# One broadcast add on VectorE and one wide absolute value in place of 16 small activations in the delta rule's decay exponent

## The chip, the cores and the metric

The kernel runs on one core of a Trainium2 chip. The core has five engines with a queue of their own each: TensorE (PE, matrix products; its weight loads are PEld), VectorE (DVE), ScalarE (ACT), GpSimd (POOL) and SyncE (SP, which issues the DMAs here). The metric is the device time of one execution in microseconds (us), less is better.

## The reference

One layer of a diffusion backbone on 1024 latent tokens and 256 context tokens of width 1024: a norm and modulation, one wide input projection, a Fourier branch and a bidirectional gated DeltaNet branch of 8 heads, gates and an output projection, then a convolutional feed-forward part. The change lies in the DeltaNet branch. Cut to that:

```python
gc = jnp.cumsum(chunks(g), axis=-1)                       # log-decay, summed within a chunk
decay = jnp.exp(jnp.where(lower_incl, gc[..., :, None] - gc[..., None, :], -jnp.inf))
l_mat = jnp.where(lower_strict, bc[..., :, None] * kk * decay, 0.0)
sol = lax.linalg.triangular_solve(l_mat, rhs, ...)        # per chunk
qk = jnp.einsum('nbhcd,nbhsd->nbhcs', qc, kc) * decay
state, o = lax.scan(step, state, (q_head, qk, u, w, k_tail, g_last))   # chunk by chunk
```

The kernel takes chunks of 128 tokens and needs, for each chunk and each of the two directions, the 128 x 128 table exp(-|gc_i - gc_j|).

## The kernel before

**Recording and planning.** The program is written as a list of operations; line 349 (`issue`) emits every one of them, so all instructions of the profile carry that line. Before that a list scheduler (`schedule`) orders them: each operation has a cost in ns by a formula (`cost`), a rank from its longest chain of followers, and the engine that comes free first takes the ready operation of the highest rank. Each engine then runs its list strictly in that order. An operation's cost, its engine and their number thus set the order of all that is recorded around it, on every queue.

**Stages.** The DeltaNet part has ten stages, in the order c0, x0, x1, c1, x2, ... x7 (`ORDER`): c0 and c1 take four heads of the context each (4 heads x 2 chunks), x0 to x7 one head of the latent tokens each (8 chunks). So a stage always has NU = 8 blocks of 128 x 128 per direction d, in one tile of 128 x 1024. One stage is

- `decay_products`: for each direction d the chunk sums are loaded as a row, broadcast over the 128 partitions, into a tile `F` (512 KB, four buffers, two per stage); for each block u an activation takes the absolute value of the row plus a bias (`gcol`, minus the chunk sums, one number per partition and block); one activation of 1024 columns takes exp(-F). Then k k^T on TensorE, times F on VectorE (`L`), and q k^T times F;
- `invert_blocks`: 62 small VectorE operations between two round trips through DRAM (`dl` out, `bl` in; `dtt` out, `k2` in);
- `merge_blocks`: some 100 small matmuls with VectorE, ScalarE and GpSimd between them, giving the inverse `N`;
- `scan_head` or `scan_ctx`: the chain over the chunks. For a latent head it needs `qh`, the query times exp of the chunk sums (one activation of 1024 columns and one VectorE product for each direction).

`decay_products` of stage i + 1 is recorded before the scan of stage i, the inverse and the merge after it. Around them stand independent products of 512 columns (projections of k, v, q, z, the gates and f: `project_kv`, `project_kq`, `sides`), which TensorE runs while a stage's chain waits. Their results leave PSUM through ScalarE (`zh...` for z, `xsv...` for v, `qT...` for q), two banks in turn. I call the stretch between the end of one scan and the start of the next a **turn**, and name it by the stage whose F is made in it. After the ten stages come the Fourier part, the merge of the branches and the feed-forward part (from about 950 us on).

The pieces that the prediction's steps touch: lines 800 to 809 (F), 811 to 814 (k k^T, bank `pd`), 1103 to 1108 (qh), 978 to 980 (k of the context, loaded back from DRAM by `kq_ctx` after `project_kv` has stored it), 1142 to 1150 (z and the gates leave PSUM).

Of the kernel before, what the change touches and what calls it, by code (L numbers as in the profile page):

```python
# [11 lines left out]
AF = mybir.ActivationFunctionType  # L12
ALU = mybir.AluOpType
# [3 lines left out]
P = 128  # L17
# [470 lines left out]
def layer(prog, a, out):  # L488
    te, ve, se, po, sp = (prog.eng[n] for n in ("PE", "DVE", "ACT", "POOL", "SP"))
# [13 lines left out]
    def ps(tag, shape, name):  # L503
        return psum.tile(shape, F32, tag=tag, name=name, bufs=PPB if tag == "pp" else 1)
# [64 lines left out]
    def dt(tag, name, shape=(P, T), dtype=F32):  # L569
        return dp.tile(list(shape), dtype, tag=tag, name=name, bufs=bufs.get(tag, 1))  # L570
# [218 lines left out]
    NU = 8  # L789
# [6 lines left out]
    def decay_products(name, kT, co, cols, growsrc, qT=None):  # L796
        rk, b2, bk, c1 = co
        gcol = cols(ngc)
        Fs, LTs = [], []
        for d in range(2):  # L800
            F_ = dt("F", f"F_{name}{d}", (P, NU, P))
            src = growsrc(d)
            Ff = F_.rearrange("p u j -> p (u j)")
            sp.dma_start(Ff.rearrange("p (a b) -> p a b", a=src.shape[1]) if len(src.shape) == 3 else Ff, src)
            for u in range(NU):
                se.activation(F_[:, u, :], F_[:, u, :], AF.Abs, bias=gcol[:, d, u:u + 1])
            se.activation(F_, F_, AF.Exp, scale=-1.0)
            Fs.append(F_)
            LTs.append(dt("LT", f"L_{name}{d}", (P, NU, P)))
        for g in range(2):  # L810
            pt = ps("pd", [P, 4, P], f"kk_{name}{g}")
            for i in range(4):
                u = g * 4 + i
                te.matmul(pt[:, i, :], kT[:, u * P:(u + 1) * P], kT[:, u * P:(u + 1) * P], start=True, stop=True)
            for d in range(2):
                for i in range(4):
                    u = g * 4 + i
                    ve.scalar_tensor_tensor(LTs[d][:, u, :], pt[:, i, :], b2[:, d, u:u + 1], Fs[d][:, u, :],
                                            op0=ALU.mult, op1=ALU.mult)
        cl = dt("CL", f"CL_{name}", (P, 2 * NU, 32))  # L820
        for b in range(4):
            se.activation(cl[bnd[b], 0:NU, :], LTs[0][bnd[b], :, bnd[b]], AF.Copy)
            ve.transpose(cl[bnd[b], NU:2 * NU, :], LTs[1][bnd[b], :, bnd[b]])
        dl = dram.tile([2 * NU, P, 32], F32, tag="dl", name=f"dl_{name}", bufs=2)
        sp.dma_start(dl.rearrange("u p j -> p u j"), cl)
        if qT is not None:
            for g in range(2):
                pt = ps("pd", [P, 4, P], f"qkp_{name}{g}")
                for i in range(4):
                    us = slice((g * 4 + i) * P, (g * 4 + i + 1) * P)  # L830
                    te.matmul(pt[:, i, :], kT[:, us], qT[:, us], start=True, stop=True)
                for d in range(2):
                    fs = Fs[d][:, 4 * g:4 * g + 4, :]
                    ve.tensor_tensor(fs, pt, fs, op=ALU.mult)
            for d in range(2):
                po.affine_select(out=Fs[d], in_=Fs[d], pattern=[[0, NU], [1 - 2 * d, P]], compare_op=ALU.is_ge,
                                 fill=0.0, base=0, channel_multiplier=2 * d - 1)
        return Fs, LTs, dl
# [188 lines left out]
    def prepare_ctx(p, kT, rk, qT, qn):  # L1027
        made = {}

        def cols(t):  # L1030
            if id(t) not in made:
                g = const.tile([P, 2, 4, 2], F32, tag=f"g_{len(made)}", name=f"g_{len(made)}{p}", bufs=2)
                po.tensor_copy(g, t[:, :, 4 * p:4 * p + 4, 8:10])
                made[id(t)] = g.rearrange("p d h c -> p d (h c)")
            return made[id(t)]
        co = coefs(f"c{p}", rk, cols)
        src = lambda d: grd3[d * 8 + 4 * p:d * 8 + 4 * p + 4, 8:10, :].rearrange(
            "(o i) c j -> o i (c j)", o=1).broadcast_to([P, 4, TC])
        return co, cols, decay_products(f"c{p}", kT, co, cols, src)
# [54 lines left out]
    def prepare_head(h, kT, rk, qT, qn):  # L1094
        def cols(t):
            return t[:, :, h, 0:8]
        co = coefs(f"x{h}", rk, cols)
        return co, cols, decay_products(f"x{h}", kT, co, cols, grow_rows(h), qT)
# [155 lines left out]
    for g4 in range(NF):  # L1254
# [12 lines left out]
        for odd in range(2):  # L1267
            ve.tensor_tensor(quad[:, 0, odd, 0:1], ft[:, 0:1], ft[:, HALF:HALF + 1],
                             op=ALU.subtract if odd else ALU.add)
# [528 lines left out]
```

## Time and profile before

| what | value |
|---|---|
| time, median of 3 runs | 2051.59 us (2049.98 to 2053.32) |
| the profiled execution | 2047.95 us, its span 2046.2 us |
| busy PE / PEld | 1953.0 us (95%) / 1570.9 us (77%) |
| busy DVE / ACT / POOL | 1363.1 us (67%) / 858.1 us (42%) / 564.0 us (28%) |
| chain that ended last | PE 71%, DVE 14%, DMA 5%, ACT 5% |
| mean granted TensorE clock | 0.979 of full speed |

Busy time is what the profiler saw an engine work; matmuls overlap each other, so 95% does not mean that TensorE does all it could. A row of the timeline gives start and length in us, the engine, the operation, output<-input (m is a tile in SBUF, p one in PSUM, d one in DRAM), the shape, how many instructions were put together (x8), and in brackets how long the engine was idle before it and whose end released it.

### The profile page before, as it was taken

To read this page: it belongs to the slowest core of one execution; us is meant where nothing else is said; L and a number is where in the kernel's file an instruction comes from. 1 tells how busy PE (TensorE), PEld (TensorE's weight loads), DVE (VectorE), ACT (ScalarE), POOL (GpSimd) and SP (SyncE) were. 2 spreads that over 40 slices of the span, in tenths; PEclk is the share of its full clock that TensorE was granted. 3 is DMA by queue.
4 is the path that set the end of the run, shared out by engine and by line. 5 is a ranking of instruction groups with operands and counts; after the bars stand their busy time and mean duration, and the time that the engine had idled before them with its cause. 6 is when DMAs were issued, how large, how long until landed. Compare 5 with 4: busy or idle time off the path is not lost.

```text
span 2046.2 us, 31495 instructions
## 1 busy us (share of the span) xinstructions
PE 1953.0 (95%) x11470; PEld 1570.9 (77%) x11470; DVE 1363.1 (67%) x2848; ACT 858.1 (42%) x2088; POOL 564.0 (28%) x573
## 2 busy tenths in 40 slices
PE   8989999899999999999999999979999999999998
PEld 3868888787777788778776778857878888878886
DVE  5648767667677577673655485479988889882132
ACT  5575354555354453632431032454444444532121
POOL 3110121101112220210221000257878888600000
PEclk9989999899999999999999999999999999999999
DMA  7153324344451543441778562312222222453231
GB/s 298 52 187 92 105 88 132 117 145 128 113 149 52 149 150 92 118 114 51 223 234 289 181 221 102 114 52 78 95 75 80 83 83 86 167 181 100 77 126 52
DMA packets 180637, 257.52 MB, mean 126 GB/s; under 512 B 75921, under 2 KB 97522, under 8 KB 180482
## 3 DMA queue, kind: packets, MB, share of 16 engines
q1 hardware_dynamic: 180482, 255.51, 39.0%
q8 instruction: 90, 1.47, 0.3%
q14 instruction: 65, 0.53, 0.1%
HBM read 194.52 MB, written 60.94 MB: 125 GB/s over the span
## 4 chain that ended last, share of the span: by engine, by line
PE 71%; DVE 14%; DMA 5%; ACT 5%; issue 2%; POOL 1%; SPq 0%; DVEq 0%; POOLq 0%; ACTq 0%
PE p L349 71%; DVE m L349 11%; ACT m L349 4%; DMA m<-d 3%; DVE p L349 3%; DMA d<-m 2%; ACT p L349 1%; POOL m L349 1%; DMA m<-in_w_ada_dram 1%; SPq L349 0%; DMA m<-in_wu_dram 0%; ACT L349 0%; DVEq L1787 0%; POOLq L1787 0%; DVEq L349 0%
## 5 line engine op out<-in xcount | busy, mean ns | idle before, releaser
L349 PE MATMUL p<-m,m 128*128 128x512 f32 (+7 forms) x11310 | 1937.8, 338 | 75.7 <-ACT m L349 31.6
L349 PEld LDWEIGHTS p<-m,m 128*128 128x128 f32 (+4 forms) x11310 | 1551.2, 174 | 452.6 <-ACT m L349 62.4
L349 DVE TENSOR_TENSOR m<-m,m 128x512 fp32r<-128x512 f32 (+27 forms) x1096 | 557.4, 523 | 253.4 <-ACT m L349 222.8
L349 ACT ACTIVATE m<-m 128x512 fp32r<-128x512 f32 (+8 forms) x649 | 411.3, 652 | 613.5 <-DMA m<-d 161.0
L349 POOL TENSOR_TENSOR m<-m,m 128x512 fp32r<-128x512 f32 (+5 forms) x338 | 449.5, 1353 | 782.6 <-DVE m L349 625.1
L349 ACT ACTIVATE m<-p 128x512 f32<-128x512 f32 (+5 forms) x510 | 221.1, 448 | 329.3 <-PE p L349 286.0
L349 DVE SCALAR_TENSOR_TENSOR m<-p,m,m 128x128 f32<-128x128 f32 (+4 forms) x488 | 203.1, 452 | 92.3 <-ACT m L349 40.9
L349 DVE SCALAR_TENSOR_TENSOR p<-m,m,p 128x512 f32<-128x512 f32 x352 | 240.1, 749 | 2.7 <-ACT p L349 0.4
L349 ACT ACTIVATE m<-p,m 128x128 f32<-128x128 f32 (+2 forms) x240 | 115.7, 495 | 184.3 <-PE p L349 179.5
L349 POOL MEMSET m<- 128x1024 f32 (+7 forms) x79 | 35.7, 460 | 381.7 <-PE p L349 224.0
L349 POOL COPY m<-m 32x256 f32<-32x256 f32 (+2 forms) x136 | 60.3, 447 | 211.5 <-DMA m<-d 173.7
L349 DVE SCALAR_TENSOR_TENSOR m<-m,m 128x512 f32<-128x512 f32 (+5 forms) x119 | 65.7, 558 | 28.6 <-ACT m L349 16.3
L349 DVE COPY m<-p 32x256 f32<-32x256 f32 (+11 forms) x116 | 42.1, 368 | 62.5 <-PE p L349 32.8
L349 DVE TENSOR_TENSOR m<-p,m 128x512 f32<-128x512 f32 (+4 forms) x91 | 57.8, 645 | 30.5 <-PE p L349 29.1
L349 DVE SCALAR_TENSOR_TENSOR m<-m,m,m 128x1024 f32<-128x1024 f32 (+2 forms) x68 | 59.6, 878 | 26.0 <-DMA m<-in_w_ada_dram 25.6
L349 DVE TENSOR_TENSOR m<-m,p 128x128 f32<-128x128 f32 (+3 forms) x117 | 53.4, 458 | 29.6 <-PE p L349 28.8
L349 ACT ACTIVATE p<-p 128x128 f32<-128x128 f32 x208 | 55.4, 266 | 25.6 <-PE p L349 23.6
L349 DVE SCALAR_TENSOR_TENSOR m<-m,p 128x512 f32<-128x512 f32 x76 | 50.7, 682 | 13.9 <-ACT m L349 7.7
L349 DVE SCALAR_TENSOR_TENSOR m<-m,m,p 128x128 f32<-128x128 f32 x128 | 42.7, 342 | 23.5 <-PE p L349 22.8
L349 ACT ACTIVATE m<-m,m 128x128 f32<-128x128 f32 (+1 forms) x168 | 54.6, 406 | 6.3 <-DMA m<-d 3.6
L349 POOL TENSOR_SCALAR_AFFINE_SELECT m<-m 128x1024 f32<-128x1024 f32 x16 | 18.9, 1199 | 100.4 <-DVE m L349 100.4
L349 DVE SCALAR_TENSOR_TENSOR m<-m 128x1 f32<-128x1 f32 (+1 forms) x25 | 4.7, 188 | 54.3 <-ACT m L349 54.2
(20 smaller groups left out, 210.3 us busy)
## 6 DMA issues: line engine op xcount, KB each, us to landing
m<-d SPq DMA_DIRECT2D x76, 512.0 KB
d<-m SPq DMA_DIRECT2D x138, 256.0 KB
m<-d SPq DMA_DIRECT2D x114, 256.0 KB
m<-in_wi_dram SPq DMA_DIRECT2D x106, 256.0 KB
m<-in_w_ada_dram SPq DMA_DIRECT2D x48, 512.0 KB
m<-in_wu_dram SPq DMA_DIRECT2D x88, 256.0 KB
m<-in_wn_dram SPq DMA_DIRECT2D x26, 512.0 KB
m<-d SPq DMA_DIRECT2D x44, 192.0 KB
```

Source lines behind the costliest of these rows:

```text
L349: return getattr(engine.real, method)(*[real(v) for v in args], **{k_: real(v) for k_, v in kw.items()})
```

## The change

For each direction of each stage, the eight activations of 128 columns (16 per stage) go. In their place one VectorE addition of 1024 columns adds `gcol`, broadcast along the 128 columns of each block, in place on F, and one activation of 1024 columns takes the absolute value. The exponential after it stays.

```diff
-            for u in range(NU):
-                se.activation(F_[:, u, :], F_[:, u, :], AF.Abs, bias=gcol[:, d, u:u + 1])
+            ve.tensor_tensor(F_, F_, gcol[:, d, :].rearrange("p (u o) -> p u o", o=1).broadcast_to([P, NU, P]), op=ALU.add)
+            se.activation(F_, F_, AF.Abs)
             se.activation(F_, F_, AF.Exp, scale=-1.0)
```

Over ten stages ScalarE has 140 instructions less and VectorE 20 more; no DMA and no matmul is added or taken away. The planner gets other costs, and so the order changes on every engine from shortly before the first stage to the end of the last one; from the middle of the products with w_dn (`mf`, line 1402) on it is the same again.

ScalarE's queue at turn x4. The 128x128 rows of x8 are the absolute values of the two F tiles (m_191, m_197), m_241 and m_267 are the two `qh` of stage x3, p_126 is the bank from which a z product leaves. Before:

```order
 L349 ACTIVATE p_173,m_1115<-p_173 128x128
 L349 ACTIVATE m_191<-m_191,m_1051 128x128 x8
 L349 ACTIVATE m_197<-m_197,m_1051 128x128 x8
 L349 ACTIVATE m_191<-m_191 128x1024
 L349 ACTIVATE m_197<-m_197 128x1024
 L349 ACTIVATE m_354<-p_173 8x128
 L349 ACTIVATE m_241<-m_241 128x1024
 L349 ACTIVATE m_267<-m_267 128x1024
 L349 ACTIVATE m_3823<-m_3884 128x512
 L349 ACTIVATE m_4380<-p_126 128x512
```

And now, on the same engine at the same turn:

```order
 L349 ACTIVATE m_241<-m_241 128x1024
 L349 ACTIVATE m_354<-p_173 8x128
 L349 ACTIVATE m_4300<-p_126 128x512
 L349 ACTIVATE m_191<-m_191 128x1024
 L349 ACTIVATE m_267<-m_267 128x1024
 L349 ACTIVATE m_197<-m_197 128x1024
 L349 ACTIVATE m_191<-m_191 128x1024
 L349 ACTIVATE m_197<-m_197 128x1024
 L349 ACTIVATE m_518<-p_124,m_328 128x512
 L349 ACTIVATE m_4300<-p_126 128x512
```

One `qh` exponential and one z product's way out of PSUM now stand ahead of all work on F, the second `qh` between the two absolute values.

VectorE's queue at the same turn, with the change. m_744 is the block inverse of stage x3, whose last step is the 128x16 row; m_241 and m_267 are the `qh` products; m_191 and m_197 are the new additions; the SCALAR_TENSOR_TENSOR on m_354 is a first step of the scan of x3, the transpose the first step of its merge:

```order
 L349 TENSOR_TENSOR m_744<-m_744,m_737 128x16
 L349 TENSOR_TENSOR m_241<-m_518,m_241 128x1024
 L349 TENSOR_TENSOR m_191<-m_191,m_1032 128x1024
 L349 TENSOR_TENSOR m_197<-m_197,m_1032 128x1024
 L349 SCALAR_TENSOR_TENSOR m_354<-p_169,m_1042,m_207 128x128
 L349 TENSOR_TENSOR m_267<-m_518,m_267 128x1024
...
 L349 STREAM_TRANSPOSE m_773<-m_423 128x512
```

Without the two additions the queue before had the same rows in the same order: the additions stand behind the finished inverse and ahead of the first scan step and the merge.

TensorE's queue at the first stage. p_97<-m_284 is k k^T of c0, which reads the loaded k; p_124 and p_126 are the two halves of the first v product. Before:

```order
 L349 MATMUL p_124<-m_115,m_479 128x512
 L349 MATMUL p_124<-m_200,m_479 128x512
 L349 MATMUL p_124<-m_115,m_507 128x512
 L349 MATMUL p_97<-m_284 128x128 x4
 L349 MATMUL p_126<-m_401,m_497 128x512
 L349 MATMUL p_126<-m_120,m_497 128x512
```

Now:

```order
 L349 MATMUL p_126<-m_91,m_507 128x512
 L349 MATMUL p_126<-m_115,m_479 128x512
 L349 MATMUL p_97<-m_284 128x128 x4
 L349 MATMUL p_126<-m_200,m_479 128x512
 L349 MATMUL p_126<-m_115,m_507 128x512
```

The k k^T products moved behind 22 of the 24 products of the second half (p_126), which they stood ahead of.

## Rows read from the trace of the kernel before

**Rows 1.** The page: busy time, and the clock in 40 slices (tenths).

```profile
PE 1953.0 (95%) x11470; PEld 1570.9 (77%) x11470; DVE 1363.1 (67%) x2848; ACT 858.1 (42%) x2088; POOL 564.0 (28%) x573
PEclk9989999899999999999999999999999999999999
```

**Rows 2.** Who waited for whom, 100 to 1100 us: total us, times, longest.

```profile
PE p L349 <- ACT m L349: 16.9, 13, 4.2
PE p L349 <- DMA m<-d: 14.3, 7, 8.7
```

**Rows 3.** Groups by shape: count | busy us, mean ns | idle before.

```profile
L349 ACT ACTIVATE m<-m,m 128x128 f32<-128x128 f32 x160 | 50.5, 397 | 3.6 <-DMA m<-d 3.6
L349 ACT ACTIVATE m<-m 128x1024 f32<-128x1024 f32 x46 | 47.1, 1056 | 10.2 <-DMA m<-d 5.0 <-DMA m<-in_x_dram 3.2 <-DMA m<-in_ctx_dram 1.8
L349 DVE TENSOR_TENSOR m<-m,m 128x1024 f32<-128x1024 f32 x36 | 44.5, 1248 | 13.0 <-ACT m L349 12.6
```

**Rows 4.** Timeline of ACT, turn x2, in order of time.

```profile
470.54 4.50 ACT L349 ACTIVATE m<-m,m 128x128 f32<-128x128 f32 x15
474.94 2.00 ACT L349 ACTIVATE m<-m 128x1024 f32<-128x1024 f32 x2
...
477.11 0.68 ACT L349 ACTIVATE m<-p,m 128x512 f32<-128x512 f32 x1
477.68 0.59 ACT L349 ACTIVATE m<-p 128x512 f32<-128x512 f32 x1
```

**Rows 5.** Timeline of PE, the same turn.

```profile
472.62 2.24 PE L349 MATMUL p<-m,m 128*128 128x512 f32 x9
478.33 2.29 PE L349 MATMUL p<-m,m 128*128 128x512 f32 x5 [3.47 <-ACT m L349]
```

**Rows 6.** Timeline of ACT, turn x4.

```profile
602.18 2.46 ACT L349 ACTIVATE m<-m,m 128x128 f32<-128x128 f32 x8 [2.69 <-DMA m<-d]
604.94 2.46 ACT L349 ACTIVATE m<-m,m 128x128 f32<-128x128 f32 x8 [0.30 <-DMA m<-d]
607.29 2.00 ACT L349 ACTIVATE m<-m 128x1024 f32<-128x1024 f32 x2
609.18 0.25 ACT L349 ACTIVATE m<-p 8x128 f32<-8x128 f32 x1
609.34 2.50 ACT L349 ACTIVATE m<-m 128x1024 f32<-128x1024 f32 x3
611.75 0.57 ACT L349 ACTIVATE m<-p 128x512 f32<-128x512 f32 x1
```

**Rows 7.** Timelines of PE and DVE, the same turn.

```profile
612.38 1.22 PE L349 MATMUL p<-m,m 128*128 128x512 f32 x2 [4.18 <-ACT m L349]
610.41 1.23 DVE L349 TENSOR_TENSOR m<-m,m 128x1024 f32<-128x1024 f32 x1 [8.90 <-ACT m L349]
```

**Rows 8.** Timelines of ACT and PE, turn x5.

```profile
674.24 4.79 ACT L349 ACTIVATE m<-m,m 128x128 f32<-128x128 f32 x16
678.92 2.01 ACT L349 ACTIVATE m<-m 128x1024 f32<-128x1024 f32 x2
681.74 2.71 PE L349 MATMUL p<-m,m 128*128 128x512 f32 x6 [2.47 <-ACT m L349]
```

**Rows 9.** The first stage: PE's timeline, then two pieces of the chain (start, us).

```profile
147.25 1.01 PE L349 MATMUL p<-m 128*128 128x128 f32 x3 [8.74 <-DMA m<-d]
132.48 8.47 DMA d<-m
141.01 5.50 DMA m<-d
```

**Rows 10.** Windows: length, PE, PEld, DVE, ACT, POOL busy (x), clock, DMA share, GB/s.

```profile
142.70:156.40 13.70, 8.63 (x27) 7.07 (x28) 6.78 (x24) 13.69 (x39) 2.45 (x3) 0.50 0.47 154
477.20:484.00 6.80, 5.67 (x14) 4.31 (x15) 4.04 (x7) 3.24 (x6) 1.64 (x1) 0.50 0.62 116
610.30:624.00 13.70, 7.93 (x139) 5.45 (x140) 6.88 (x11) 4.37 (x9) 6.46 (x12) 0.50 0.29 75
682.00:685.40 3.40, 3.40 (x9) 2.68 (x9) 1.75 (x3) 2.15 (x4) 1.90 (x2) 0.50 0.72 154
```

**Rows 11.** Timeline of DVE: two wide products one behind the other.

```profile
398.35 2.36 DVE L349 TENSOR_TENSOR m<-m,m 128x1024 f32<-128x1024 f32 x2
```

## Prediction

> **What bounds the kernel now.** The page comes first: TensorE is busy for 95% of the span, VectorE for 67%, ScalarE for 42% [rows 1]. So an edit on ScalarE and VectorE moves the end only where TensorE waits for them, and the whole prize lies in TensorE's idle time and in the stretches in which its clock is down. The view of waits for 100 to 1100 us, where the ten stages run, says how much that is: TensorE waited 16.9 us for ScalarE's tiles and 14.3 us for loads from DRAM [rows 2]. Next, the timelines at the longest of these waits. Three of the ScalarE waits, 3.47, 4.18 and 2.47 us, together 10.1 us, fall in the turns x2, x4 and x5 [rows 5, 7, 8], and in each ScalarE is in the middle of the very activations that the change takes out: 15 or 16 absolute values in a row of 4.5 to 4.9 us, and two exponentials of 2.0 us behind them [rows 4, 6, 8]. TensorE waits there for nothing in F; it waits for a PSUM bank, and the activation that empties it (477.11 and 477.68, 611.75) is queued behind F [rows 4, 6]. The longest load wait, 8.74 us, is k k^T of the first stage: the store of k took 8.47 us, and loading it back 5.50 [rows 9]. Last the windows: after four of these waits the granted clock reads 0.50, the lower of the two levels, for 13.7, 6.8, 13.7 and 3.4 us, with TensorE busy for 8.63, 5.67, 7.93 and 3.40 us of them [rows 10]; half of such busy time is lost.
>
> **What each edit costs.** Durations first. Fifteen absolute values end to end take 4.50 us, one alone 0.397, so one takes (4.50 - 0.40) / 14 = 0.293 us of ScalarE's time [rows 3, 4] and eight take 2.34. A wide one without bias takes 2.00 - 1.06 = 0.94 us when another follows [rows 3, 4]. ScalarE so saves 2.34 - 0.94 = 1.40 us per direction, 20 x 1.40 = 28 us in all. No row shows a VectorE addition with this broadcast; the nearest are its products of 1024 columns, 1.25 us in the mean and 2.36 - 1.23 = 1.13 end to end [rows 3, 7, 11]. I take 1.25: VectorE gains 20 x 1.25 = 25 us. Latency on one tile hardly moves: 2.34 + 0.94 before, 1.25 + 0.94 + 0.94 and a hand-over now. So F isn't ready sooner; what changes is how long ScalarE is shut for others.
>
> One rule of the Trainium skill speaks against the edit. The rows price a biased absolute value of 128 columns at 0.293 us of queue time [rows 3, 4]. In "ScalarE: Activation LUTs", section "What ACT_TABLE_LOAD costs", a bias read per partition adds about 93 ns to an activation: an estimate by that page makes the bias itself worth 160 x 0.093 = 15 us of ScalarE in all. By that sum alone the change would buy an addition of 15 us on one engine with 25 us on another. The rows include what that sum leaves out, that seven of eight fixed costs go too, and no run here has shown the bias apart.
>
> *The three turns.* At x2 and x5, 16 absolute values and two exponentials shut ScalarE for 6.3 to 6.7 us [rows 4, 8]. By the order, three wide activations (2.8 us) now stand ahead of the first bank's exit at x2, and at x4 and x5 one z exit stands ahead of all of F. x2: 6.3 - 2.8 = 3.5 us earlier, of a wait of 3.47; I take -3.0. x4: the exit at 611.75 waited for the landing of F (2.69 and 0.30 us), for F and for two `qh` [rows 6]; one exit is now free of that, the second isn't, and the first `qh` product, for which VectorE sat 8.90 us [rows 7], can run before F lands. I take -3.5 of 4.18. x5: -2.0 of 2.47. Together -8.5; bounds 0 (the banks fill again at once, the second exit waits as before) and -10.1.
>
> *The clock behind them.* TensorE was busy 5.67 + 7.93 + 3.40 = 17.0 us at the lower level [rows 10]; if none of it came back, 8.5 us would be won. I take half, -4; bounds 0 and -8.5.
>
> *The opening.* k k^T moves behind 22 products of 512 columns. Nine take 2.24 us, the last alone some 0.4, so one takes 0.23 [rows 5] and 22 take 5.1. Against that, one addition now stands on VectorE between the second and third pieces of the key that must be stored: +1.25, if its row has landed by then. Net -3.9, I take -4. Bounds: 0 (the store and the load land as much later) and, with the clock after it, -8.7 - 8.63 / 2 = -13.0 [rows 9, 10].
>
> *The additions' place.* At x4, x5 and x6 they stand behind the finished inverse, where VectorE before sat idle 8.90 us [rows 7]; that wait is their cover, and there I cost them at nothing. At c1, x2 and x3 they stand amid a merge, an inverse and a scan: two additions each delay such a chain by 2 x 1.13 = 2.3 us [rows 11]. I charge two of the three, +4.5. Bounds 0 and, all 20 uncovered, +25. Where a row lands late (2.69 + 0.30 us at x4 [rows 6]) VectorE is now held as well, and ScalarE behind it; as the rest of the order is also new, I charge one such landing, +3, bounds 0 and +9 for three. SyncE issues the same transfers; nothing there is dearer.
>
> **Sum.** -8.5 - 4 - 4 + 4.5 + 3 = -9.0 us. The profiled execution took 2047.95 us, 1.75 more than its span, and would take 2039.0; it lies 3.6 us under the median of 2051.59. From the median the forecast is **2042.6 us**. The bounds added up would be -31.6 and +34; they don't all meet.
>
> **The rivals.** *No change: loads set the turns.* At x4 F landed at 602.18 and 604.94 [rows 6], later than ScalarE wanted it. If the landings and not ScalarE's queue decide, the waits stay, first on VectorE and then on ScalarE; then only x2 is won (-3.0), the +3 takes it back, and the opening stays as it is: 0, or about 2051.6. For it: 14.3 us of waits for loads [rows 2]. Against: at x2 and x5 the absolute values ran without a wait for a load [rows 4, 8].
>
> *Slower: VectorE's queue is the one that is late.* VectorE runs in order; an addition that waits for its row holds the scan's first step and the merge's transpose behind it, and the merge ends the stage. Price: 2.3 us for a stage, and 3.0 for a late landing. It decides from where VectorE's idle time in a turn is under 2.3 us. If five of the ten stages lose their 2.3, two of them wait for a landing too, half of the three turns' gain and the opening's stay and the clock gives nothing back: 11.5 + 6.0 - 4.25 - 4 = +9.25, or 2060.8. For it: VectorE was busy 67% [rows 1], ScalarE only 42. Against: the 8.90 us of VectorE idle at the turn [rows 7]. What this rests on is also stated by the Trainium skill, "Perfetto Trace Analysis", section "Per-engine timelines": the queues of ScalarE, VectorE and GpSimd are strictly first in, first out. The trace agrees: at 602.18 ScalarE had sat 2.69 us before one load, and nothing behind it ran [rows 6].
>
> *Faster still: the opening closes.* If the first load lands before TensorE reaches k k^T, its 8.74 us and the low clock go with it: -13.0 in place of -4, 2033.6.
>
> That the change doesn't do what it says is out: the order shows the wide operations in place of the small ones.
>
> **How the numbers follow.** Forecast (2036 to 2047.4) 0.45, opening closed (2028 to 2036) 0.15, loads set the turns (2047.5 to 2055.7) 0.20, VectorE late (2055.7 to 2070) 0.20. 0.2% is 4.1 us, about what a measurement of this kernel can tell from no change: faster by more 0.60, within 0.20, slower 0.20. The range of 8 in 10 leaves out the lower part of the opening's case (0.06) and the upper part of the slow one (0.13): 2031 to 2059.
>
> **What the profile after would show.** Right: ScalarE about 28 us less busy and VectorE 25 us more; 20 additions of 1.1 to 1.4 us; no ScalarE wait of TensorE over 2.5 us at x2, x4 and x5, the `qh` product of x3 before F's addition; less time at the lower clock between 477 and 685 us; the first long wait under 6 us. Wrong: TensorE's waits for VectorE's tiles grow by as much as those for ScalarE's shrink, or additions with several us of idle ahead of them for a load while a transpose or scan step stands behind; or new waits for loads at places where before had none, since the whole list was planned anew. The last would make the prediction wrong without touching its reasons, and is the reason why the range is wide.

## The result, and the profile after

The changed kernel takes **2031.31 us** (median of 4 runs, 2029.80 to 2035.48) against 2052.45 for the kernel before beside it: a ratio of **0.9896, 95% interval 0.9878 to 0.9915**, some 21 us less. The forecast was 2042.6, with a range of 2031 to 2059. The direction was right, the gain was more than twice the 9.0 us forecast, and the time lies at the very edge of the range. The profiled execution took 2029.80 us, span 2028.1.

The page of the kernel after: busy time and the clock in 40 slices. It answers to [rows 1].

```profile
PE 1947.3 (96%) x11470; PEld 1566.6 (77%) x11470; DVE 1383.4 (68%) x2868; ACT 829.1 (41%) x1948; POOL 560.0 (28%) x573
PEclk9999999899999999999999999999999999999999
```

ScalarE is 29.0 us less busy (forecast 28), VectorE 20.3 us more (25). TensorE's waits from 100 to 1100 us, after, answer to [rows 2]:

```profile
PE p L349 <- ACT m L349: 15.0, 18, 2.4
PE p L349 <- DVE m L349: 10.6, 16, 2.3
PE p L349 <- ACT p L349: 8.2, 5, 4.1
PE p L349 <- DMA m<-d: 2.0, 3, 1.1
```

No wait for ScalarE's tiles in SBUF (the m) is over 2.4 us, yet their total fell only from 16.9 to 15.0 us: the three turns fell by 4.3 us (10.1 to 5.8), and waits at other places grew. The waits for loads fell from 14.3 to 2.0 us, and 4.1 us of that came back at the opening as a wait for ScalarE (ACT p). The turns, after; first x2, ACT and then PE, for [rows 4, 5]:

```profile
471.08 3.10 ACT L349 ACTIVATE m<-m 128x1024 f32<-128x1024 f32 x3 [0.45 <-DVE m L349]
474.08 0.67 ACT L349 ACTIVATE m<-p,m 128x512 f32<-128x512 f32 x1
474.65 1.04 ACT L349 ACTIVATE m<-m 128x1024 f32<-128x1024 f32 x1
475.60 0.58 ACT L349 ACTIVATE m<-p 128x512 f32<-128x512 f32 x1
476.23 6.12 PE L349 MATMUL p<-m,m 128*128 128x512 f32 x19 [2.31 <-ACT m L349]
```

Three wide activations stand ahead of the first bank's way out of PSUM (its exit, for short), as the prediction read from the order, and a fourth between it and the second exit (475.60), with whose end the wait ends. TensorE still waits 2.31 us, of 3.47. Turn x4, ACT and then PE, for [rows 6, 7]:

```profile
611.11 0.60 ACT L349 ACTIVATE m<-p 128x512 f32<-128x512 f32 x1 [0.89 <-PE p L349]
612.53 1.06 ACT L349 ACTIVATE m<-m 128x1024 f32<-128x1024 f32 x1 [0.82 <-DVE m L349]
613.81 3.90 ACT L349 ACTIVATE m<-m 128x1024 f32<-128x1024 f32 x4 [0.22 <-DMA m<-d]
...
618.81 0.59 ACT L349 ACTIVATE m<-p 128x512 f32<-128x512 f32 x1
619.28 1.34 ACT L349 ACTIVATE m<-m 128x512 fp32r<-128x512 f32 x2
...
611.76 5.81 PE L349 MATMUL p<-m,m 128*128 128x512 f32 x24 [0.69 <-ACT m L349]
619.97 1.06 PE L349 MATMUL p<-m,m 128*128 128x512 f32 x2 [2.40 <-ACT m L349]
```

One exit (611.11) is ahead of all of F, so 24 more products run. The second (618.81) stands behind five wide activations; what TensorE then waits 2.40 us for is the conversion of 128x512 right behind that exit (the first of the two at 619.28), whose end releases the products at 619.97. Turn x5, PE, for [rows 8]: the 2.47 us are 0.39.

```profile
678.43 10.45 PE L349 MATMUL p<-m,m 128*128 128x512 f32 x44 [0.39 <-ACT m L349]
```

The opening, PE, for [rows 9]: k k^T (the 128x128 rows) starts at 150.46 without a wait, behind the 22 products; the wait is 4.12 us, ahead of these products and for a PSUM tile of ScalarE, where it was 8.74 for the load.

```profile
142.68 7.94 PE L349 MATMUL p<-m,m 128*128 128x512 f32 x22 [4.12 <-ACT p L349]
150.46 1.05 PE L349 MATMUL p<-m 128*128 128x128 f32 x8
```

**Where the 21 us are.** To compare kernels whose orders differ, the traces were laid side by side by work done: TensorE's busy time, the part of it at the granted clock of 0.50 counted half. For each stretch of the kernel before, the table has how much more (+) or less (-) time the other kernel took for the same amount of work, that is the difference in idle time plus half the difference in busy time at 0.50. It is worked out from one profiled execution of each kernel. After and e1 have the same TensorE queue from end to end, and yet differ by 3.3 us in the last row; before and e2 also have one queue, and differ by 5.5 us from 850 to 1200. Taken alone, a row of a few us is no more than a hint. The row 490 to 600 is left out (0.3 us at most); some 1.4 us of a span stay unexplained. The other columns belong to the experiments below.

| stretch of before, us | after | e1 | e2 | e3 | e4 | e12 | e11 |
|---|---|---|---|---|---|---|---|
| 0 to 160, opening | -5.8 | -3.3 | -0.7 | -7.8 | -2.1 | +0.6 | -1.4 |
| 160 to 430, x0, x1, c1 | +5.9 | +5.2 | +0.2 | +4.0 | +0.3 | -0.5 | -1.7 |
| 430 to 490, x2 | -2.5 | +1.0 | +3.0 | +0.4 | -2.1 | -2.0 | +1.1 |
| 600 to 640, x4 | -6.7 | -6.1 | -1.5 | -0.4 | -5.7 | -5.4 | +0.3 |
| 640 to 700, x5 | -3.9 | -4.2 | -2.0 | -1.3 | -4.3 | -3.9 | -3.6 |
| 700 to 800, x6 | +1.2 | +4.2 | -0.7 | -0.7 | +0.9 | +0.5 | +1.9 |
| 800 to 850, x7 | -3.7 | -2.9 | +1.3 | +1.1 | -3.9 | -3.5 | +0.9 |
| 850 to 1200 | -3.8 | -3.2 | +5.5 | +3.2 | -3.5 | +2.1 | +3.2 |
| 1200 to 2000 | -0.1 | +3.2 | 0.0 | +3.4 | +0.3 | -0.2 | +0.1 |

So after: the opening wins 5.8 us, and all of it is lost again by 430 us; the three turns win 13.1; a further 7.5 come at x7 and up to 1200 us, where the prediction had nothing. The sum is 19.5 us; the spans of these two executions differ by 18.1, the medians by 21.

### The profile page after: what moved, and what is told of

It reads as the page before. It is cut to its first block, busy times and chain, and to the rows that moved or that the text cites. A ratio compares the mean times of both kernels' runs of the same rounds, so it can differ in the third digit from the quotient of the medians.

```text
span 2028.1 us, 31373 instructions
## 1 busy us (share of the span) xinstructions
PE 1947.3 (96%) x11470; PEld 1566.6 (77%) x11470; DVE 1383.4 (68%) x2868; ACT 829.1 (41%) x1948; POOL 560.0 (28%) x573
## 4 chain that ended last, share of the span: by engine, by line
PE 75%; DVE 11%; DMA 5%; ACT 4%; issue 2%; POOL 1%; SPq 0%; DVEq 0%; POOLq 0%; ACTq 0%
PE p L349 75%; DVE m L349 9%; ACT m L349 3%; DVE p L349 3%; DMA d<-m 2%; DMA m<-d 2%; POOL m L349 1%; ACT p L349 0%; SPq L349 0%; DMA m<-in_wu_dram 0%; ACT L349 0%; DVEq L1787 0%; POOLq L1787 0%; ACTq L349 0%; DVEq L349 0%
## 5 line engine op out<-in xcount | busy, mean ns | idle before, releaser
L349 PE MATMUL p<-m,m 128*128 128x512 f32 (+5 forms) x11310 | 1933.7, 337 | 72.9 <-ACT m L349 28.1
L349 PEld LDWEIGHTS p<-m,m 128*128 128x128 f32 (+3 forms) x11310 | 1548.6, 173 | 449.5 <-ACT m L349 64.6
L349 DVE TENSOR_TENSOR m<-m,m 128x512 fp32r<-128x512 f32 (+22 forms) x1116 | 579.6, 535 | 236.3 <-ACT m L349 207.7
L349 ACT ACTIVATE m<-m 128x512 fp32r<-128x512 f32 (+8 forms) x669 | 431.7, 663 | 636.0 <-DMA m<-d 165.5
L349 POOL COPY m<-m 32x256 f32<-32x256 f32 (+2 forms) x136 | 54.6, 404 | 202.8 <-DMA m<-d 156.6
L349 DVE TENSOR_TENSOR m<-m,p 128x128 f32<-128x128 f32 (+3 forms) x117 | 53.6, 459 | 23.1 <-PE p L349 22.4
L349 ACT ACTIVATION_READ_ACCUMULATOR p<-p 128x1 f32 x208 | 39.5, 190 | 0.0
L349 ACT ACTIVATE p<-m,m 128x512 f32<-128x512 f32 x44 | 30.3, 691 | 21.6 <-DVE m L349 21.2
```

Source lines behind the costliest of these rows:

```text
L349: return getattr(engine.real, method)(*[real(v) for v in args], **{k_: real(v) for k_, v in kw.items()})
```

## The experiments

Theories at the start: W, the shorter work on F opens the turns; O, the order that the planner now writes does it; and for the opening, that its gain stays or is given back. The change does two things at once, since the planner gets other costs: other operations, and another order. e1 and e2 part them. Both let the planner see one form and issue the other.

### e1 and e2: the order without the work, the work without the order

```diff
 # e1: planned as the changed kernel; at issue, for each pair
-ve.tensor_tensor(F_, F_, gcol..., op=ALU.add); se.activation(F_, F_, AF.Abs)
+for u in range(8): se.activation(F_[:, u, :], F_[:, u, :], AF.Abs, bias=gcol[:, d, u:u + 1])
 # e2: planned as the kernel before; at issue
-the first of eight small absolute values, ..., the last
+the addition on VectorE,                  ..., the wide absolute value
```

> The planner still sees the addition and the wide absolute value, so the order of every engine is that of the changed kernel; but at issue each pair becomes the eight biased absolute values of 128 columns again, at the wide one's place on ScalarE, and VectorE adds nothing. Theory W (the shorter ScalarE work opens the turns): the three turns x2, x4 and x5 and the clock behind them come back, about -13 of the -21 us are lost, and the kernel takes 2044 to 2050 us against about 2052 of the kernel before; TensorE's ScalarE waits at x2, x4, x5 are again 2.5 us or more. Theory O (the new order does it, whatever the work on F costs): 2030 to 2036 us, waits as in the changed kernel.

> The other half: the planner sees the eight biased absolute values, so all other instructions stand in the order of the kernel before; at issue the first of the eight becomes the addition on VectorE and the last the wide absolute value on ScalarE. Theory W: at x2 and x5 ScalarE is free 2.8 us sooner and at x4 too unless the loads decide, so 2036 to 2044 us. Theory O: 2048 to 2054 us, since k k^T and the bank exits stay where they were, and above that (up to 2062) if the addition, which stands on VectorE at a place that was not planned for it, holds the chain behind it.

e1 took 2041.40 us, ratio 0.9959 (0.9944 to 0.9974); e2 took 2054.90, ratio 1.0031 (1.0020 to 1.0041). The new order alone wins 8 us, the new work alone loses 5 to 6, both together win some 20. Neither W nor O: each half needs the other. What the change costs where the order isn't made for it shows in ACT and PE of e2 at turn x2:

```profile
477.18 2.95 ACT L350 ACTIVATE m<-m 128x1024 f32<-128x1024 f32 x3 [2.71 <-DVE m L350]
...
480.32 0.67 ACT L350 ACTIVATE m<-p,m 128x512 f32<-128x512 f32 x1
480.89 0.58 ACT L350 ACTIVATE m<-p 128x512 f32<-128x512 f32 x1
...
481.52 2.71 PE L350 MATMUL p<-m,m 128*128 128x512 f32 x6 [4.83 <-ACT m L350]
```

ScalarE sits 2.71 us ahead of the wide absolute value, since the addition stands in VectorE's queue behind work that was planned there without it (VectorE has no gap from 468 to 480 us); both exits (480.32, 480.89) stand behind, and TensorE's 3.47 us are 4.83. This is the rival "VectorE's queue is late". The Trainium skill, "Perfetto Trace Analysis", section "Per-engine timelines", has the queues of ScalarE and VectorE as strictly first in, first out; this row agrees.

x2 (+3.0 us in the table) is not all of e2's loss: x4 and x5 win 3.5 there, and the largest loss, 5.5 us, lies from 850 to 1200, behind x7. PE there, before and then e2:

```profile
906.77 77.66 PE L349 MATMUL p<-m,m 128*128 128x512 f32 x509 [0.44 <-issue]
```

```profile
909.90 79.18 PE L350 MATMUL p<-m,m 128*128 128x512 f32 x509 [2.52 <-issue]
```

The queue is the same; the wait is 2.1 us longer, and from 900 to 950 us e2 has 3.4 us of its products at the lower clock, where before has none. The profile names nothing that the wait is for, so why it is longer stays open.

e1 parts the turns (ACT, then PE; x2, then x4):

```profile
477.42 2.43 ACT L350 ACTIVATE m<-m,m 128x128 f32<-128x128 f32 x8
479.76 0.67 ACT L350 ACTIVATE m<-p,m 128x512 f32<-128x512 f32 x1
480.33 1.04 ACT L350 ACTIVATE m<-m 128x1024 f32<-128x1024 f32 x1
481.27 0.58 ACT L350 ACTIVATE m<-p 128x512 f32<-128x512 f32 x1
...
481.90 4.37 PE L350 MATMUL p<-m,m 128*128 128x512 f32 x11 [4.52 <-ACT m L350]
...
617.50 0.60 ACT L350 ACTIVATE m<-p 128x512 f32<-128x512 f32 x1 [0.78 <-PE p L350]
617.99 2.44 ACT L350 ACTIVATE m<-m,m 128x128 f32<-128x128 f32 x8
...
618.15 5.82 PE L350 MATMUL p<-m,m 128*128 128x512 f32 x24 [0.69 <-ACT m L350]
627.24 4.99 PE L350 MATMUL p<-m,m 128*128 128x512 f32 x112 [3.27 <-ACT m L350]
```

At x2 the small values, back in the new order, bring the wait to 4.52 us: there the shorter work is the gain. At x4 the exit at 617.50 is ahead of F and the 24 products run, with the small values behind it: there the order is the gain (-6.1 of -6.7 us in the table), and the work adds 0.9 us (3.27 against 2.40).

### e3 and e4: the first three stages, and the last seven

```diff
+if name in ("c0", "x0", "x1"):    # e4: ("c1", "x2", ..., "x7")
     ve.tensor_tensor(F_, F_, gcol..., op=ALU.add); se.activation(F_, F_, AF.Abs)
+else:
+    for u in range(NU): se.activation(F_[:, u, :], F_[:, u, :], AF.Abs, bias=gcol[:, d, u:u + 1])
```

> The addition and the wide absolute value in the stages c0, x0 and x1 alone, the eight small ones in the other seven, planned with these. The trace of the changed kernel is 5.8 us ahead at 160 us and has lost all of it by 410 us. Theory 1 (the opening's gain is given back in the waits of x0 and c1): -1 to +2 us against the kernel before, so 2050 to 2055, with a first long wait of about 4 us instead of 8.7. Theory 2 (the opening's gain stays; what the changed kernel loses up to 410 us is the price of c1's additions): -4 to -7, 2045 to 2049.

> The complement: the new form in c1 and x2 to x7, the small ones in c0, x0 and x1. By theory 1 the whole gain is here: 2031 to 2036 us, with the first long wait of 8.7 us as in the kernel before. By theory 2 the opening's 5 to 6 us are missing: 2036 to 2041.

e3: 2046.84 us, ratio 0.9992 (0.9980 to 1.0004); e4: 2031.07, ratio 0.9911 (0.9896 to 0.9926). In us, e3 lies in theory 2's interval, but the kernel before took 2049.45 beside it: by the ratio the difference is 1.6 us (0.8 more to 4.1 less), between the two theories and not to be told from none. e4 decides for theory 1: the gain of the changed kernel is there, 18 us of 21 by the ratios, whose intervals overlap, in the last seven stages alone, with an opening's wait of 8.62 us. So of the opening's 7.8 us in e3 little or nothing is left at the end. In the table 4.0 of them are gone by 430 us; most of the rest goes behind 850 us, in rows that differ as much between equal queues. The additions aren't what takes it back: up to 430 us e1, which has none, loses 5.2 us, and e4, with the new form in c1, 0.3. In the table the kernels that win over 3 us at the opening (after, e1, e3) lose 4 us or more up to 430, and the others 0.3 at most. The loss can be seen in the windows from 250 to 300 us, of before and then of after (PE busy and its count first), each with its products of 512 columns:

```profile
250.00:300.00 50.00, 47.77 (x467) 39.59 (x466) 35.95 (x94) 24.98 (x84) 11.35 (x18) 1.00 0.30 88
L349 PE MATMUL p<-m,m 128*128 128x512 f32 x111 | 29.7, 405 | 0.8 <-DVE m L349 0.8
```

```profile
250.00:300.00 50.00, 44.97 (x443) 36.97 (x442) 35.52 (x101) 24.20 (x83) 11.46 (x20) 0.97 0.37 112
L349 PE MATMUL p<-m,m 128*128 128x512 f32 x85 | 24.3, 427 | 2.5 <-ACT p L349 1.9 <-DVE m L349 0.6
```

TensorE's timeline of after in that stretch, an inverse and its merge:

```profile
284.90 1.75 PE L349 MATMUL p<-m,m 128*128 128x128 f32 x38 [0.30 <-ACT m L349]
287.06 1.79 PE L349 MATMUL p<-m,m 64*64 64x64 f32 x36 [0.41 <-DVE m L349]
289.01 2.88 PE L349 MATMUL p<-m,m 128*128 128x128 f32 x40 [0.16 <-DVE m L349]
...
295.56 4.62 PE L349 MATMUL p<-m,m 128*128 128x512 f32 x13 [1.86 <-ACT p L349]
```

and of before:

```profile
262.75 27.36 PE L349 MATMUL p<-m,m 128*128 128x512 f32 x351 [0.78 <-DVE m L349]
```

Before, products of 512 columns ran among the small ones for 27 us without a gap; after, 85 of them are left in the 50 us where 111 were, and the inverse runs bare, waiting from step to step. Counted by their starts in the traces, the kernel before has begun 355 products of 512 columns at 160 us, 627 at 250, 736 at 300 and 904 at 400 us; after has begun 384, 640, 725 and 904. The products that filled the opening are independent work taken from a fixed stock: 29 ahead at 160 us, 11 behind at 300, level at 400. That the missing ones here are those very 22 wasn't shown.

### e5 and e6: other plans for either form

A rival to all of this is luck: any new plan may move the time. Two numbers of the planner that have nothing to do with F were changed, each with both forms.

```diff
-("ACT", "PE"): 281
+("ACT", "PE"): 300        # e5_before_lat, e6_after_lat
-MIX = 0.1
+MIX = 0.105               # e5_before_mix, e6_after_mix
```

> The kernel before (small absolute values), with one number of the planner changed that has nothing to do with F: the latency that it assumes from ScalarE to TensorE, 300 ns in place of 281. 2681 of TensorE's 9401 instructions stand elsewhere. Theory F (the gain comes from an order that fits the shorter ScalarE work): any plan for the small ones keeps ScalarE shut for 4.5 to 6.7 us at the turns, so 2045 to 2055 us. Theory L (luck of the draw: any new plan moves the time by 10 us and more, and the changed kernel got a good one): the time may well be off by over 8 us in either direction, as 2035 or 2065.

> The changed kernel with the same number of the planner changed, 300 ns for 281 (2023 of TensorE's instructions stand elsewhere). Theory F: the gain over its partner with the small absolute values under the same number stays at 14 to 26 us, so about 2026 to 2038. Theory L: the gain falls under 10 us, 2040 to 2050.

> The kernel before with another number of the planner changed: the weight that it gives to the recorded order, 0.105 for 0.1 (2639 of TensorE's instructions stand elsewhere). Theory F: 2045 to 2055 us. Theory L: over 8 us from the kernel before in either direction.

> The changed kernel with the weight 0.105 for 0.1 (2700 of TensorE's instructions stand elsewhere). Theory F: 14 to 26 us under its partner with the small absolute values and the same weight. Theory L: less than 10 us under it, or above it.

| planner | small form | wide form | wide less small |
|---|---|---|---|
| as it was | 2052.45 | 2031.31 | -21.1 |
| latency 300 | 2045.85 | 2029.37 | -16.5 |
| weight 0.105 | 2044.80 | 2027.71 | -17.1 |

Ratios to the kernel before: 0.9962 (0.9946 to 0.9978), 0.9891 (0.9870 to 0.9912), 0.9966 (0.9950 to 0.9982), 0.9880 (0.9863 to 0.9896). Luck falls as the explanation: under three plans the wide form wins 16 to 21 us. But a plan is worth 6 to 8 us by itself to the small form (to the wide one at most 4, with intervals that overlap), and of the three the kernel before had the poorest (e5_before_mix, at 2044.80, came out just under the 2045 to 2055 that theory F gave it): the other two pairs differ by 16.8 in the mean, so some 4 of its 21 us may be that. It is a rough figure, since the kernel before itself took 2049.45 to 2052.45 beside the different experiments, and 2051.61 here. The turn x4 shows the tie between form and order: -5.5 to -4.8 us in the two wide kernels here, -1.7 and -1.6 in the two small ones. At x5 it doesn't: e5_before_lat wins 4.1 us there with small values.

### e7, e9 and e8: the price of the addition, and of the bias

All three keep the changed kernel's order to the instruction.

```diff
 ve.tensor_tensor(F_, F_, gcol..., op=ALU.add)      # e9: left out
+ve.tensor_tensor(F_, F_, F_, op=ALU.max)           # e7 only
-se.activation(F_, F_, AF.Abs)                      # e8 only
+for u in range(8): se.activation(F_[:, u, :], F_[:, u, :], AF.Abs)
```

> The changed kernel in its own order, with a second VectorE operation of 1024 columns (the maximum of F with itself) right behind each of the 20 additions; about 22.6 us more VectorE work, 1.13 us for each. Theory C (the additions are covered: VectorE waits at the turns anyway): within 3 us of the changed kernel, 2028 to 2034 us. Theory X (additions amid a merge or a scan are exposed, as the prediction charged for two stages of ten): +4.5 us or more, 2035.8 and up; all 20 exposed would give 2054.

> The changed kernel in its own order without the 20 additions: the absolute value is taken of F alone, so the bias is left out of the computation. ScalarE's wide absolute value waits for the load itself. Theory C: within 3 us of the changed kernel, 2028 to 2034. Theory X: about 4.5 us less, 2027 and below.

> The changed kernel in its own order with the addition on VectorE, but the wide absolute value taken as eight of 128 columns without a bias. It parts the bias from the number of instructions. If the bias read per partition is what made the small ones dear (the Trainium skill's 93 ns, as an estimate: 0.293 - 0.093), one takes 0.20 us end to end, eight 1.6, ScalarE has 13 us more than in the changed kernel and the time lies halfway to the run with the eight biased ones in the same order, 2034 to 2038 us. If the bias costs nothing, one takes 0.29 us, ScalarE has 28 us more, and the time is that of that run, 2039 to 2044.

Without the additions (so the bias is left out of the exponent): 2028.42 us, ratio 0.9892 (0.9878 to 0.9907), 2.9 under the changed kernel, with intervals that overlap: 20 additions of 1.22 us cost some 0 to 3 us. With a second operation behind each: 2044.26, ratio 0.9969 (0.9956 to 0.9982), 13 us more than the changed kernel (15 by the ratios), for 25.7 us more of VectorE's busy time. So both theories are right, each for one step: the order has cover for one addition and not for a second. The waits of ScalarE's wide activations (the end of the row: idle ahead, by cause), after and then e7, tell why; the ones for VectorE grew from 8.4 to 22.4 us:

```profile
L349 ACT ACTIVATE m<-m 128x1024 f32<-128x1024 f32 x66 | 67.9, 1052 | 26.6 <-DMA m<-d 12.9 <-DVE m L349 8.4 <-DMA m<-in_x_dram 3.2
```

```profile
L350 ACT ACTIVATE m<-m 128x1024 f32<-128x1024 f32 x66 | 68.1, 1053 | 39.6 <-DVE m L350 22.4 <-DMA m<-d 11.9 <-DMA m<-in_x_dram 3.1
```

e8 took 2037.63 us, ratio 0.9933 (0.9914 to 0.9951), some 60% of the way to e1, in the range of the bias theory. Turn x2 of e8, ACT and then PE; the 17 are 16 absolute values with one wide exponential among them, and the exits behind them are left out:

```profile
473.98 4.39 ACT L350 ACTIVATE m<-m 128x128 f32<-128x128 f32 x17 [0.46 <-DVE m L350]
...
480.43 3.88 PE L350 MATMUL p<-m,m 128*128 128x512 f32 x10 [3.62 <-ACT m L350]
```

From start to start, one such absolute value takes 200 ns without the bias and 292 with it (medians of 141 each, in e8 and e1): the bias is 92 ns, 14.7 us in 160; the other half of ScalarE's 29 us is the number of instructions, and that alone (e8 to after) is worth 6 to 8 us of the time here. The Trainium skill, "ScalarE: Activation LUTs", section "What ACT_TABLE_LOAD costs", has about 93 ns for an operand read per partition; the measurement agrees. In one order, the wait at x2 so follows what stands ahead of the exit: 1.75 us without additions, 2.31 after, 3.62 with eight plain values, 4.12 with a second operation on VectorE, 4.52 with eight biased ones.

### e10: two good variants together

```diff
 # e4, and
-MIX = 0.1
+MIX = 0.105
```

> The new form in the last seven stages alone, planned with the weight 0.105 for the recorded order: the two variants that came out at or under the changed kernel, together. If the planner's draw adds to the gain, 2026 to 2030 us; if draws are independent of each other, anywhere from 2026 to 2036.

2031.38 us, ratio 0.9903 (0.9887 to 0.9920): nothing gained; what a plan is worth doesn't carry from one to the next. e6_after_mix has the lowest median of all, 2027.71, with an interval that overlaps the changed kernel's.

### e12 and e11: where the late gain comes from

```diff
+if name in ("c1", "x2", "x3", "x4", "x5"):    # e11: ("x6", "x7")
```

> The new form in c1 and x2 to x5 alone, the small absolute values in c0, x0, x1, x6 and x7. By the traces, the changed kernel gains 13 us in the turns x2, x4, x5 and another 6 to 7 from 800 us on (the wait at 823 us, and waits up to 1200 us), which the prediction has no term for. Theory T (the late gain belongs to the new form in the late stages x6 and x7): about 13 us under the kernel before, 2035 to 2041, with the 2 us wait near 820 still there. Theory P (it belongs to the planner's list as a whole, which differs from the first turns on): about 19 under it, 2029 to 2035, without that wait.

> The new form in the last two stages x6 and x7 alone; everything up to the turn x6 stands as in the kernel before. Theory T: the late gain of 6 to 7 us is here and the 13 us of the turns are not, 2042 to 2047 us, and the wait near 823 us is gone. Theory P: within 3 us of the kernel before, or slower, 2047 to 2055, with the wait.

e12: 2038.39 us, ratio 0.9940 (0.9921 to 0.9960); e11: 2049.95, ratio 0.9995 (0.9981 to 1.0010). Five stages win 11 to 12 us, two win nothing, the seven together some 18 (e4). Neither theory holds whole. e11's queues differ from those of the kernel before from 668 us on, within turn x5, sooner than its expectation has it. The wait near 820 us (2.06 us in the kernel before), in PE's timeline of e11 and then of e12:

```profile
824.12 4.54 PE L349 MATMUL p<-m,m 32*32 32x32 f32 x140 [1.95 <-DMA m<-d]
```

```profile
824.31 0.38 PE L349 MATMUL p<-m 128*128 128x128 f32 x2
...
825.90 0.90 PE L349 MATMUL p<-m,m 32*32 32x32 f32 x4 [0.29 <-DMA m<-d]
```

e11 has the wide form at x7 itself and keeps the wait; e12 has the small form there and is rid of it. So the 3.7 us at x7 belong to the order that follows from the earlier turns, and T falls there. The part from 850 to 1200 us is in neither e11 nor e12 (+3.2 and +2.1 us) and in all kernels whose list was planned for the wide form in all seven (after, e1, e4: -3.2 to -3.8; the two of e6: -1.9 and -2.3). That e11 and e12 are slower there than the kernel before can't be read from this: e2, with the queue of the kernel before, reads +5.5. The gain goes with the order, since e1 has it with the small values; what in the order brings it stays open.

## Why the prediction was right or wrong, step by step

The steps that failed are three terms of the sum: the charges for the additions (+4.5 and +3, together 7.5 us, for 0 to 3 measured), the opening (-4, booked as won, and about nothing in the end), and the stages behind x5, which had no term and gave 6.4 us. The three turns came out as forecast in sum.

**What bounds the kernel: right.** TensorE's idle time fell by 12.4 us (span less busy time, 93.2 to 80.8) and its busy time by 5.7; it was busy at the lower clock for 14.1 us less (58.3 to 44.2), half of which is 7.0.

**The durations: right.** ScalarE -29.0 us for -28; the additions 1.22 us each, for 1.25; VectorE's total grew by 20.3, less than 20 x 1.22.

**The three turns and the clock behind them: right in sum, not in their parts.** Forecast -8.5 and -4; measured, in the table's way, -7.8 us of idle time (x2 -1.3, x4 -4.4, x5 -2.1) and -5.3 of clock: -13.1 for -12.5. x2 was taken at -3.0 and gave 1.3: the wait ends with the second exit (475.60), with a fourth wide activation ahead of it, not with the first; the kernel before had its wait end with the second one too (477.68 in [rows 4], released at 478.28). (The rows shut ScalarE for 6.4 us there, not 6.3.) x4 gave more than -3.5, and for the reason that the prediction read from the order, one exit ahead of F, which e1 shows apart from the work. x5 happened, but isn't tied to the form: e11 and e5_before_lat win it with small values there.

**The opening: the first step that failed.** At the place itself the term was near (-4 forecast, -5.8 measured), but the prediction booked it as won. By e3 and e4 it can't be told from 0. What was missing is where the work that fills the hole is taken from: products moved forward are missing later (29 ahead at 160 us, 11 behind at 300).

**The charges: the second step that failed, +4.5 and +3.** By e9 all 20 additions cost 2.9 us by the medians and 0.8 by the ratios, and the late landing that was to hold VectorE didn't come: 0.5 us of waiting for loads ahead of VectorE's wide additions and products, in this group of after:

```profile
L349 DVE TENSOR_TENSOR m<-m,m 128x1024 f32<-128x1024 f32 x56 | 67.7, 1222 | 6.3 <-ACT m L349 5.5 <-DMA m<-d 0.5
```

By these waits the planner had put the additions where their rows had landed; e2 shows at x2 what such an addition costs without a place of its own in the plan. Opening and charges together were +3.5 us in the sum and are 0.1 in the trace (-5.8 and +5.9 up to 430 us).

**What had no term: the largest error.** x7 and the stretch up to 1200 us, 7.5 us, less 1.2 lost at x6. The prediction said that "the whole list was planned anew" and took it for a risk only, with +3 as its size. By the runs another plan takes 6 to 8 us off the small form and at most 4 off the wide one, and the wide form gives late gains that no single stage owns (e11 0, e12 11 to 12, e4 18). At x7 e12 shows that they come with the order of the earlier turns; up to 1200 us their cause stays open. What the prediction named as signs of being right came out (VectorE 20.3 us more for 25); none of them looked behind x5. The sum of the errors: 0.6 us at the turns, 3.4 for opening and charges, 6.4 after 700 us: together 10.4 of the 10.5 by which the table's -19.5 differs from -9.0 (the spans differ by 18.1; 1.4 us is what the table leaves over).

**The rivals.** "Loads set the turns": no, load waits fell from 14.3 to 2.0 us. "VectorE's queue is late": not in the changed kernel (TensorE's waits for it fell from 14.2 to 10.6 us), but it is what e2 shows at x2. "The opening closes": it didn't, and 2033.6 came near the measured time for another reason.

## What to carry to other kernels

When a list is planned by costs, an edit changes the work and the order, and the two can be told apart by planning one and issuing the other; here -8 us, +5 to 6 us and, together, -20. A stall that is filled with independent work was a loan here: look for the place where that work was before, and book the gain only if TensorE had cover to spare there. Before reading a few tenths of a per cent as the effect of an edit, plan the kernel before two more times with a number that doesn't matter.

## What the runs showed of the hardware

A bias read per partition costs ScalarE 92 ns of queue time in an absolute value of 128 columns, nearly half of the 200 that it takes without one.

The same products in the same order didn't get the same clock. From 1310 to 1480 us TensorE's queue in after and in e1 holds the same products; aligned by their first wait, the windows of after and then of e1 read a granted clock of 0.96 and 0.93, the mean of stretches at 1.00 and at 0.50:

```profile
1310.00:1480.00 170.00, 149.20 (x623) 116.17 (x622) 151.16 (x200) 77.64 (x140) 122.39 (x93) 0.96 0.22 74
```

```profile
1321.00:1491.00 170.00, 150.50 (x613) 117.47 (x612) 153.49 (x200) 75.91 (x138) 119.51 (x91) 0.93 0.21 73
```

In e1 23.9 us of them lie at 0.50 and in after 13.7, although most waits differ by hundredths (2.02 and 2.04, 1.88 and 1.89, 1.82 and 1.82, 2.63 and 2.64 us; one is shorter in e1, 0.51 for 1.14 us, behind products that ran at the lower clock). This lies behind the +3.2 us of e1's last row in the table: the clock term of a sum can't be trusted to less than that here.
